# A hybrid encoder layer on one core: the first loads in wider pieces, four pool tiles accumulated together, stored tiles read back through POOL's queue

## The chip, the cores and the metric

The kernel runs on one core of one Trainium2 chip. The time is the device time of one execution in microseconds. A core has a matmul engine (TensorE, PE in the profile, with PEld for its weight loads), a vector engine (VectorE, DVE), a scalar engine (ScalarE, ACT), GpSimd (POOL) and SyncE (SP). In this kernel SP and POOL issue the transfers between DRAM and on-chip memory. Products accumulate in PSUM; a PSUM slot here holds 128 rows of 512 floats.

## The reference

One layer is computed for T = 384 tokens: 256 of one new stream and 8 x 16 of eight running streams. All data is float32.

```python
u = rmsnorm(x, g_mix_pre)
proj = u @ w_in                                  # pool | z | xBC | dt | gates
a_pool = pool_mixer(proj[pool])                  # windows 2, 4, 8, 16: mean minus self, then a map per group of 512
xbc = silu(causal_conv(proj[xBC]))
y, h = ssd_scan(xbc, softplus(proj[dt]))         # exact chunked scan
a_ssd = gated_rmsnorm(y + d_skip * x, z)
m = sigmoid(g_A) * (a_pool @ w_pool_proj) + sigmoid(g_B) * (a_ssd @ w_ssd_proj)
x = x + rmsnorm(m @ w_out, g_mix_post)
x = x + rmsnorm(relu(rmsnorm(x, g_mlp_pre) @ w_up)**2 @ w_down, g_mlp_post)
```

The model width is 2048 (KD = 16 tiles of 128), the SSD branch is 4096 wide in 8 groups, the MLP 8192. The new pool, convolution and SSM states are outputs as well.

## The kernel before

**Products in three parts.** A float32 product is made of three products in a rounded format: each operand is split into a rounded high part `h` (ScalarE, an activation with Copy) and the rest `l` (VectorE, a subtraction), and `mm3` (L75) adds h·h, h·l and l·h. So each weight piece passes one transfer on SP, one split on ScalarE, one on VectorE, and then TensorE.

**Weight units.** `wfetch` (L59) brings one unit, 128 rows of 1024 floats (512 KB), `wsplit` (L64) splits it. The pool `wpool` has three buffers each for the raw unit, its high and its low part. `proj` (L104) makes one tile of 128 output columns x 384 tokens from two units, in the two `mmtile` slots of PSUM; `moving` (L110) makes three token blocks x 512 output columns in three of the six `sstile` slots, from units of 18 products of 512 columns each. `take` (L95) hands out a split unit: as long as the list `queue` isn't empty, it keeps three split units in `ready`, so that a split is ordered two units ahead of its use; with an empty list it orders load and split where they are used.

**What sets the order.** The framework orders the instructions of each engine when the program is built, by the order of the code as priority and by when its model says that an instruction can run. On the chip each engine then takes its own list strictly in that order, and waits on semaphores. `behind` pins single instructions behind others. Tiles of one name share a fixed number of slots; a new tile waits until the old one has been read for the last time.

**The opening (L196 to L312).** Eight products on zeros (`NWARM`, L200) run while the first loads are on their way. x is loaded transposed, one tile of 128 x 384 for each k (`xload`, L213), the weights of the first three pool tiles as `w_e`, 384 columns for each k (`eload`, L208): k=0 and k=1 alone, then pairs, through the weight buffers of `wpool`. `xsplit` (L239) splits x times the norm's gain, `esplit` (L252) the weights, and `eprod` (L263) adds the products of k into three PSUM slots. The fourth pool tile, `ps3`, is then made from two ordinary units (`f0`, `f1`). x is loaded a second time by tokens (`tload`) for the row norms: three squares on ScalarE, three Newton steps on VectorE, and two products (`bc_x`, L309) that spread the norms over the partitions; ScalarE copies them to `rstd` (L311). Until then no pool tile can leave PSUM.

**The pooling stage (L329 to L496).** `pool_tile` reads a tile from PSUM, scales it by `rstd`, forms the window sums on VectorE, and splits the result. `pool_map` multiplies four of these tiles by the group's weights. Between them stand the first gates (`gate_a`): the first is made after the pool tile (1, 0). Here is the order:

```python
for gi in range(4):
    for k4 in range(4):
        pool_tile(gi, k4)
        if gi and k4 == 0:
            if gi == 1:
                sg = gate_a(0)
            pool_map(gi - 1, last[0])
```

The gated results `ma_scr` and the second gates `gb_scr` go to DRAM through POOL's queue, as do the 32 tiles of the SSD branch, `a_scr` (L783).

**The SSD groups (L792 to L881)** take their units, and those of the second gates (`w_gb`), from `queue`, which L796 and L797 fill.

**The branch projection, the merge and the output (L883 to L1091).** While the last two gates (`gate_b(2)` and `gate_b(3)`, L917) run, `aload` (L907) is called after each unit: it brings two tiles of `a_scr` back through SP's queue into three buffers named `ar`, and splits them on ScalarE (L913) and VectorE (L914). Then, for each of four blocks of 512 columns, `ma_scr` and `gb_scr` are read back through SP's queue (L925, L926), the branch is projected with 16 units of `w_ssd`, and the three are merged. `w_out` follows with 8 units for each block; in its last block five units have buffers of their own.

**The MLP (L1094 to L1251)** ends with `w_down`. `moving`'s arguments `tail` and `own` there: in the very last block all four units are used block by block (`tail` = 4), and one of them is split into buffers of its own rather than into those of `wpool` (`own` = 1). The last block of tokens is then normed, added to x and stored (L1223 to L1241).

Of the kernel before, what the change touches and what calls it, by code (L numbers as in the profile page):

```python
# [6 lines left out]
F32 = mybir.dt.float32  # L7
F32R = mybir.dt.float32r
# [6 lines left out]
P = 128  # L15
# [10 lines left out]
MAGIC = 1597463007.0  # L26
NWARM = 8

# [5 lines left out]
def build(ctx, tc, io):  # L34
# [148 lines left out]
    def in_units(i):  # L183
        return [win[i - 4, 0], win[i - 4, 1]]

# [10 lines left out]
    warm = pa.tile([P, 512], mybir.dt.bfloat16, name="warm", bufs=1)  # L196
    gp.memset(warm, 0.0)
    gp.memset(onesr.bitcast(F32), 1.0)
# [3 lines left out]

    x0 = pa.tile([P, KD + T], F32, name="x0g", bufs=1)
    sy.dma_start(x0, io["x0g"])
# [12 lines left out]

# [14 lines left out]
    f0 = wfetch(in_units(4)[0], "p3_0")  # L232
    sy.dma_start(ident, io["cst"][:, C_IDENT : C_IDENT + P])
    tload(2)
    f1 = wfetch(in_units(4)[1], "p3_1")
    sy.dma_start(cst[:, P:], io["cst"][:, P:])
    sy.dma_start(vec, io["vec"])

    def xsplit(k):  # L239
        x = xr[k]  # L240
        h = xgp.tile([P, T], F32R, name=f"xgh{k}")
        l = xgp.tile([P, T], F32R, name=f"xgl{k}")
        g1 = x0[:, k : k + 1]
        s.activation(h, x, AF.Copy, scale=g1)
        v.scalar_tensor_tensor(out=l, in0=x, scalar=g1, in1=h.bitcast(F32), op0=ALU.mult, op1=ALU.subtract)
        xg.append((h, l))

    early = [sstile(f"pj_p{n}")[:, :T] for n in range(3)]

    turn = [None]  # L250

    def esplit(k):  # L252
        w, n = eu[k]
        h = wpool.tile([P, 1024], F32R, tag="wh", name=f"wh_e{k}")[:, : n * T]
        l = wpool.tile([P, 1024], F32R, tag="wl", name=f"wl_e{k}")[:, : n * T]
        if k == 0:
            v.tensor_copy(h, w)
        else:
            turn[0] = s.activation(h, w, AF.Copy)
        v.tensor_tensor(l, w, h.bitcast(F32), ALU.subtract)  # L260
        return h, l

    def eprod(k, j, hl):  # L263
        h, l = hl
        col = lambda n: slice(j * T + n * P, j * T + n * P + P)
        xh, xl = xg[k]
        if k == 0:
            for a, b in ((h, xh), (h, xl), (l, xh)):
                for n in range(3):
                    te.matmul(early[n], a[:, col(n)], b, start=a is h and b is xh, stop=False)  # L270
            return
        for n in range(3):
            last[0] = mm3(early[n], h[:, col(n)], l[:, col(n)], xh, xl, False, k == KD - 1)
# [6 lines left out]

    for k in (0, 1):
        hl = esplit(k) if k == 0 else None
        xsplit(k)
        eprod(k, 0, hl or esplit(k))
    for k in range(2, KD, 2):
        xsplit(k)
        xsplit(k + 1)
        hl = esplit(k)
        eprod(k, 0, hl)
        eprod(k + 1, 1, hl)  # L290
        if k in (10, 14):
            square((k - 10) // 4, turn[0])
    ps3 = sstile("pj_p3")[:, :T]
    early.append(ps3)
    half(ps3, 0, wsplit(f0), xg)
    square(2, None)
    half(ps3, 1, wsplit(f1), xg)
    dgh = pa.tile([P, 3, P], F32R, name="dgh", bufs=1)
# [17 lines left out]
    with tc.tile_pool(name="phc", bufs=1, reuse_waits="tile") as pc, tc.tile_pool(name="phc2", bufs=2, reuse_waits="tile") as pc2:  # L316
# [192 lines left out]
    with tc.tile_pool(name="phd", bufs=2, reuse_waits="tile") as pd, tc.tile_pool(  # L509
# [391 lines left out]
    with ExitStack() as phe:  # L901
        pe1 = phe.enter_context(tc.tile_pool(name="phe", bufs=1, reuse_waits="tile"))
        pe2 = phe.enter_context(tc.tile_pool(name="phe2", bufs=3, reuse_waits="tile"))
        pe4 = phe.enter_context(tc.tile_pool(name="phe4", bufs=1, reuse_waits="tile"))
        ab = []

        def aload():  # L907
            for i in (len(ab), len(ab) + 1):
                a = pe2.tile([P, T], F32, tag="ar", name=f"ar{i}")
                sy.dma_start(a, a_scr[i])  # L910
                h = pe1.tile([P, T], F32R, name=f"abh{i}")
                l = pe1.tile([P, T], F32R, name=f"abl{i}")
                s.activation(h, a, AF.Copy)  # L913
# [278 lines left out]
    with tc.tile_pool(name="phg", bufs=1, reuse_waits="tile") as pg, tc.tile_pool(  # L1192
# [9 lines left out]
        for c8 in range(NC):  # L1202
# [12 lines left out]
            for nb in range(4):  # L1215
                o = [sstile(f"wd{c8}_{nb}_{b}") for b in range(3)]

                def done(b):
# [154 lines left out]
```

## Time and profile before

| | |
|---|---|
| three runs, median (lowest to highest) | 2807.32 us (2806.77 to 2808.29) |
| the profiled execution | 2807.07 us |
| its span in the profile | 2804.9 us |
| mean granted clock of TensorE | 0.999 |
| read from DRAM, written | 407.11 MB, 41.72 MB |

The profile shows one execution. Times are microseconds from the span's start unless marked ns. A row of the timeline gives start, duration, engine, line of the kernel, operation, output and inputs, shapes, how many were merged into the row, and in brackets how long the engine was idle ahead of it and what ended that. Rows of waits give the waiting engine and line, whom it waited for, the total in us, how often and the longest. A row of groups gives the count, the busy time, the mean in ns of one, and the idle time ahead. A row of transfers gives the issuing queue, the count, the size of one and the median time from issue to landing. A row of stretches gives start and end, length, then for each engine the busy time and the instructions, then granted clock, busy share of the transfer engines and GB/s. Ends of products are modelled, so rows of PE overlap; the distance of two starts is what a product costs.

### The profile page before, as it was taken

How to read it: one execution, taken by the hardware profiler on the slowest of the kernel's cores; microseconds unless marked ns; L12 is line 12 of the kernel's file. 1: busy time of each engine (PE TensorE's matmuls, PEld its weight loads, DVE VectorE, ACT ScalarE, POOL GpSimd, SP SyncE). 2: the span in 40 equal slices, each digit the busy share in tenths (PEclk: the TensorE clock that was granted, in tenths of full speed). 3: DMA queues.
4: the chain of work that ended last, by engine and by line, in shares of the span. 5: the costliest groups of instructions: out<-in, count | busy, mean ns of one | idle time of the engine just before them, and what ended most of it. 6: DMA issues, size and time to landing. Idle time of an engine off the chain costs nothing.

```text
span 2804.9 us, 38300 instructions
## 1 busy us (share of the span) xinstructions
PE 2792.9 (100%) x15271; PEld 2542.6 (91%) x15271; DVE 1501.4 (54%) x1979; ACT 1173.4 (42%) x1822; POOL 105.8 (4%) x143
## 2 busy tenths in 40 slices
PE   9999999999999999999999999999999999999998
PEld 8998889999999999988888888989899898989897
DVE  6575335677787778756333336434444444444446
ACT  5443225556565656544322235433233332323233
POOL 0000000001010101010000000000000000000000
PEclk9999999999999999999999999999999999999999
DMA  7444445556665566657544544443444443444443
GB/s 272 131 124 150 139 139 199 186 182 207 197 228 192 201 198 223 197 186 233 175 146 161 176 144 131 130 131 125 131 126 129 127 130 126 129 128 128 130 127 124
DMA packets 148355, 451.35 MB, mean 161 GB/s; under 512 B 18064, under 2 KB 49104, under 8 KB 143184
## 3 DMA queue, kind: packets, MB, share of 16 engines
q1 hardware_dynamic: 140048, 412.97, 45.9%
q0 software_dynamic: 8128, 35.93, 3.3%
q8 instruction: 120, 1.97, 0.3%
q14 instruction: 59, 0.48, 0.1%
HBM read 407.11 MB, written 41.72 MB: 160 GB/s over the span
## 4 chain that ended last, share of the span: by engine, by line
PE 98%; ACT 1%; DMA 0%; DVE 0%; issue 0%; SPq 0%; DVEq 0%; ACTq 0%
PE pj_up L77 6%; PE pj_up L78 6%; PE pj_up L76 6%; PE wd L120 6%; PE wd L118 6%; PE wd L119 6%; PE pj_x L76 5%; PE pj_x L78 4%; PE pj_x L77 4%; PE pj_z L76 3%; PE pj_z L77 3%; PE pj_z L78 3%; PE pj_sp L119 3%; PE pj_sp L120 3%; PE pj_sp L118 3%; PE pj_gb L118 2%
## 5 line engine op out<-in xcount | busy, mean ns | idle before, releaser
L77 PE MATMUL pj_up<-x1l,wh_up 128*128 128x384 f32 (+1 forms) x1032 | 343.9, 333 | 0.6 <-DVE x1l L1041 0.6
L76 PE MATMUL pj_up<-x1h,wh_up 128*128 128x384 f32 (+1 forms) x1032 | 344.0, 333 | 0.0
L78 PE MATMUL pj_up<-x1h,wl_up 128*128 128x384 f32 (+1 forms) x1032 | 343.9, 333 | 0.0
L120 PE MATMUL wd<-wh_wd,hl 128*128 128x512 f32 x762 | 296.6, 389 | 0.0
L119 PE MATMUL wd<-wl_wd,hh 128*128 128x512 f32 x762 | 296.6, 389 | 0.0
L118 PE MATMUL wd<-wh_wd,hh 128*128 128x512 f32 x762 | 296.3, 389 | 0.0
L69 DVE TENSOR_TENSOR wl_wd<-w_wd,wh_wd 128x1024 fp32r<-128x1024 f32 x127 | 155.7, 1226 | 261.9 <-ACT wh_wd L68 261.9
L68 ACT ACTIVATE wh_wd<-w_wd 128x1024 fp32r<-128x1024 f32 x127 | 134.8, 1061 | 350.8 <-PE wd L120 284.2
L68 ACT ACTIVATE wh_up<-w_up 128x1024 fp32r<-128x1024 f32 x126 | 133.7, 1061 | 322.1 <-PE pj_up L77 258.0
L69 DVE TENSOR_TENSOR wl_up<-w_up,wh_up 128x1024 fp32r<-128x1024 f32 x126 | 154.4, 1226 | 198.1 <-ACT wh_up L68 198.0
L76 PE MATMUL pj_x<-xgh,wh_x 128*128 128x384 f32 x768 | 258.2, 336 | 0.0
L77 PE MATMUL pj_x<-xgl,wh_x 128*128 128x384 f32 x768 | 256.6, 334 | 0.0
L78 PE MATMUL pj_x<-xgh,wl_x 128*128 128x384 f32 x768 | 256.6, 334 | 0.0
L77 PEld LDWEIGHTS pj_up<-x1l,wh_up 128*128 128x128 f32 x1032 | 193.8, 188 | 1.0 <-DVE x1l L1041 0.7
L76 PEld LDWEIGHTS pj_up<-x1h,wh_up 128*128 128x128 f32 x1032 | 193.7, 188 | 0.3
L78 PEld LDWEIGHTS pj_up<-x1h,wl_up 128*128 128x128 f32 x1032 | 193.8, 188 | 0.0
L78 PE MATMUL pj_z<-xgh,wl_z 128*128 128x384 f32 x512 | 171.0, 334 | 0.0
L76 PE MATMUL pj_z<-xgh,wh_z 128*128 128x384 f32 x512 | 171.0, 334 | 0.0
L77 PE MATMUL pj_z<-xgl,wh_z 128*128 128x384 f32 x512 | 171.0, 334 | 0.0
L120 PEld LDWEIGHTS wd<-wh_wd,hl 128*128 128x128 f32 x762 | 143.0, 188 | 29.8
L119 PEld LDWEIGHTS wd<-wl_wd,hh 128*128 128x128 f32 x762 | 143.0, 188 | 29.7
L118 PEld LDWEIGHTS wd<-wh_wd,hh 128*128 128x128 f32 x762 | 143.0, 188 | 29.4
(319 smaller groups left out, 5799.7 us busy)
## 6 DMA issues: line engine op xcount, KB each, us to landing
w_up<-w_up SPq DMA_DIRECT2D x128, 512.0 KB, 3.4
w_wd<-w_down SPq DMA_DIRECT2D x128, 512.0 KB, 3.4
w_x<-w_in SPq DMA_DIRECT2D x96, 512.0 KB, 3.8
w_z<-w_in SPq DMA_DIRECT2D x64, 512.0 KB, 3.9
w_sp<-w_ssd SPq DMA_DIRECT2D x64, 512.0 KB, 3.4
w_ga<-w_ga SPq DMA_DIRECT2D x32, 512.0 KB, 3.5
w_pp<-w_pp SPq DMA_DIRECT2D x32, 512.0 KB, 3.4
hs<-ssm SPq DMA_DIRECT2D x16, 1024.0 KB, 5.4
```

Of the source, the lines that this page charges most:

```text
L68: s.activation(h, w, AF.Copy)
L69: v.tensor_tensor(l, w, h.bitcast(F32), ALU.subtract)
L76: te.matmul(out, wh, xh, start=first, stop=False, **how)
L77: te.matmul(out, wh, xl, start=False, stop=False, **how)
L78: return te.matmul(out, wl, xh, start=False, stop=last, **how)
L118: te.matmul(o[b], mh, wh[:, c], start=k == 0, stop=False)
L119: te.matmul(o[b], mh, wl[:, c], start=False, stop=False)
L120: last[0] = te.matmul(o[b], ml, wh[:, c], start=False, stop=k == nk - 1)
```

## The change

It has five parts.

1. **Opening.** x and the first weights come in one array: for each k 384 columns of x and 512 weight columns, side by side in one row of 896 floats. k=0 is one array with the gains, brought by two transfers; k=1 to 3 have a transfer and a tile each; then two transfers fill one tile of two k. The tiles have places of their own and no longer use `wpool`. Seven products on zeros instead of eight; VectorE clears their operand instead of POOL. For k=0 VectorE makes the low part of x ahead of that of the weights.
2. **Pool tiles.** The opening adds into four PSUM slots instead of three; the tile that comes from two ordinary units is the fifth, `ps4`. The first gate and the first pool map move behind the pool tile (1, 1).
3. **Queue of the loads.** The `a_scr`, `ma_scr` and `gb_scr` tiles are read back through POOL's queue instead of SP's.
4. **Splits ahead.** The units of `w_ssd` and `w_out` (but for the last five) join `queue`.
5. **End.** Two units of the last `w_down` block have buffers of their own.

```diff
-NWARM = 8
+NWARM = 7
...
-        return [win[i - 4, 0], win[i - 4, 1]]
+        return [win[i - 5, 0], win[i - 5, 1]]
...
-    gp.memset(warm, 0.0)
+    XW = T + 512
+    x0 = pa.tile([P, 928], F32, name="x0g", bufs=1)[:, : KD + XW]
+    sy.dma_start(x0[:, : KD + T], io["xw0"][:, : KD + T])
+    sy.dma_start(x0[:, KD + T :], io["xw0"][:, KD + T :])
+    v.memset(warm, 0.0)
...
-    xr.append(x0[:, KD:])
-    eu, xs3 = {}, []
-
-    def eload(k, n):
-        w = wpool.tile([P, 1024], F32, tag="w", name=f"w_e{k}")[:, : n * T]
-        sy.dma_start(w.rearrange("p (k n) -> p k n", k=n), io["w_e"][k : k + n].rearrange("k p n -> p k n"))
-        eu[k] = w, n
-
-    def xload(k):
-        x = pa.tile([P, T], F32, name=f"x{k}", bufs=1)
-        sy.dma_start(x, io["xT"][k])
-        xr.append(x)
+    xr.append(x0[:, KD : KD + T])
+    eu, xs3 = {0: x0[:, KD + T :]}, []
+
+    def xload(k, n):
+        x = pa.tile([P, n, XW], F32, name=f"xw{k}", bufs=1)
+        for j in range(n):
+            sy.dma_start(x[:, j], io["xw"][k + j])
+            xr.append(x[:, j, :T])
+        eu[k] = x[:, 0, T:] if n == 1 else x[:, :, T:]
...
-    eload(0, 1)
-    xload(1)
-    eload(1, 1)
-    for k in range(2, KD, 2):
-        xload(k)
-        xload(k + 1)
-        eload(k, 2)
+    for k in (1, 2, 3):
+        xload(k, 1)
+    for k in range(4, KD, 2):
+        xload(k, 2)
         if k in (6, 10):
             tload(len(xs3))
...
-    early = [sstile(f"pj_p{n}")[:, :T] for n in range(3)]
+    early = [sstile(f"pj_p{n}")[:, :T] for n in range(4)]
...
+        xl = None
         if k == 0:
-            v.tensor_copy(h, w)
+            v.tensor_copy(hv, w)
+            xl = xsplit(0)
         else:
-            turn[0] = s.activation(h, w, AF.Copy)
-        v.tensor_tensor(l, w, h.bitcast(F32), ALU.subtract)
+            turn[0] = s.activation(hv, w, AF.Copy)
+        with behind(xl):
+            v.tensor_tensor(lv, w, hv.bitcast(F32), ALU.subtract)
...
-                for n in range(3):
+                for n in range(4):
                     te.matmul(early[n], a[:, col(n)], b, start=a is h and b is xh, stop=False)
...
-    for k in (0, 1):
-        hl = esplit(k) if k == 0 else None
-        xsplit(k)
-        eprod(k, 0, hl or esplit(k))
-    for k in range(2, KD, 2):
+    for k in range(4):
+        if k:
+            xsplit(k)
+        eprod(k, 0, esplit(k))
+    for k in range(4, KD, 2):
         xsplit(k)
         xsplit(k + 1)
...
-            ps = early[k] if k < 4 else proj(in_units(1 + k), xg, f"p{k}")
+            ps = early[k] if k < 5 else proj(in_units(1 + k), xg, f"p{k}")
...
-                if gi and k4 == 0:
+                if gi and k4 == (gi == 1):
...
+        queue.extend((io["w_ssd"][nb, kp], f"sp{nb}_{kp}") for nb in range(4) for kp in range(16))
+        queue.extend((io["w_out"][nb, kp], f"wo{nb}_{kp}") for nb in range(4) for kp in range(8 if nb < 3 else 3))
...
-                sy.dma_start(a, a_scr[i])
+                gp.dma_start(a, a_scr[i])
...
-            sy.dma_start(ma, ma_scr[nb])
-            sy.dma_start(gb, gb_scr[nb])
+            gp.dma_start(ma, ma_scr[nb])
+            gp.dma_start(gb, gb_scr[nb])
...
-                    1 if c8 == NC - 1 and nb == 3 else 0,
+                    2 if c8 == NC - 1 and nb == 3 else 0,
...
-    cols = [i * P for i in range(3, 16)]
+    cols = [i * P for i in range(4, 16)]
...
-        "x0g": np.concatenate([chan(a["g_mix_pre"][0]), xcat[:, :P].T], axis=1),
-        "w_e": np.ascontiguousarray(w_in[:, :T]).reshape(KD, P, T),
+        "xw0": np.concatenate([chan(a["g_mix_pre"][0]), xcat[:, :P].T, w_in[:P, :512]], axis=1),
+        "xw": np.concatenate([xcat.T.reshape(KD, P, T), w_in[:, :512].reshape(KD, P, 512)], axis=2),
```

More of the change, by code (lines that the diff above doesn't have):

```diff
@@ L201, in build @@
         te.matmul(wt, warm[:, :P], warm, start=True, stop=True)
-    x0 = pa.tile([P, KD + T], F32, name="x0g", bufs=1)
-    sy.dma_start(x0, io["x0g"])
-    xr.append(x0[:, KD:])
-    eu, xs3 = {}, []
-    def eload(k, n):
-        w = wpool.tile([P, 1024], F32, tag="w", name=f"w_e{k}")[:, : n * T]
-        sy.dma_start(w.rearrange("p (k n) -> p k n", k=n), io["w_e"][k : k + n].rearrange("k p n -> p k n"))
-        eu[k] = w, n
-    def xload(k):
-        x = pa.tile([P, T], F32, name=f"x{k}", bufs=1)
-        sy.dma_start(x, io["xT"][k])
-        xr.append(x)
+    xr.append(x0[:, KD : KD + T])
[6 more added lines that the diff above has]
+        eu[k] = x[:, 0, T:] if n == 1 else x[:, :, T:]
     def tload(b):
@@ L221, in tload @@
         xs3.append(x)
-    eload(0, 1)
-    xload(1)
-    eload(1, 1)
-    for k in range(2, KD, 2):
-        xload(k)
-        xload(k + 1)
-        eload(k, 2)
+    for k in (1, 2, 3):
+        xload(k, 1)
+    for k in range(4, KD, 2):
+        xload(k, 2)
         if k in (6, 10):
             tload(len(xs3))
-    f0 = wfetch(in_units(4)[0], "p3_0")
+    f0 = wfetch(in_units(5)[0], "p4_0")
     sy.dma_start(ident, io["cst"][:, C_IDENT : C_IDENT + P])
     tload(2)
-    f1 = wfetch(in_units(4)[1], "p3_1")
+    f1 = wfetch(in_units(5)[1], "p4_1")
     sy.dma_start(cst[:, P:], io["cst"][:, P:])
@@ L244, in xsplit @@
         s.activation(h, x, AF.Copy, scale=g1)
-        v.scalar_tensor_tensor(out=l, in0=x, scalar=g1, in1=h.bitcast(F32), op0=ALU.mult, op1=ALU.subtract)
         xg.append((h, l))
-    early = [sstile(f"pj_p{n}")[:, :T] for n in range(3)]
+        return v.scalar_tensor_tensor(
+            out=l, in0=x, scalar=g1, in1=h.bitcast(F32), op0=ALU.mult, op1=ALU.subtract
+        )
+    early = [sstile(f"pj_p{n}")[:, :T] for n in range(4)]
     turn = [None]
     def esplit(k):
-        w, n = eu[k]
-        h = wpool.tile([P, 1024], F32R, tag="wh", name=f"wh_e{k}")[:, : n * T]
-        l = wpool.tile([P, 1024], F32R, tag="wl", name=f"wl_e{k}")[:, : n * T]
+        w = eu[k]
+        n = 1 if k < 4 else 2
+        h = wpool.tile([P, 1024], F32R, tag="wh", name=f"wh_e{k}")[:, : n * 512]
+        l = wpool.tile([P, 1024], F32R, tag="wl", name=f"wl_e{k}")[:, : n * 512]
+        hv, lv = (h, l) if n == 1 else (a.rearrange("p (k n) -> p k n", k=2) for a in (h, l))
+        xl = None
         if k == 0:
-            v.tensor_copy(h, w)
-        else:
-            turn[0] = s.activation(h, w, AF.Copy)
-        v.tensor_tensor(l, w, h.bitcast(F32), ALU.subtract)
+            v.tensor_copy(hv, w)
+            xl = xsplit(0)
+        else:
+            turn[0] = s.activation(hv, w, AF.Copy)
+        with behind(xl):
+            v.tensor_tensor(lv, w, hv.bitcast(F32), ALU.subtract)
         return h, l
@@ L264, in eprod @@
         h, l = hl
-        col = lambda n: slice(j * T + n * P, j * T + n * P + P)
+        col = lambda n: slice(j * 512 + n * P, j * 512 + n * P + P)
         xh, xl = xg[k]
@@ L268, in eprod @@
             for a, b in ((h, xh), (h, xl), (l, xh)):
-                for n in range(3):
+                for n in range(4):
                     te.matmul(early[n], a[:, col(n)], b, start=a is h and b is xh, stop=False)
             return
-        for n in range(3):
+        for n in range(4):
             last[0] = mm3(early[n], h[:, col(n)], l[:, col(n)], xh, xl, False, k == KD - 1)
@@ L292, in build @@
             square((k - 10) // 4, turn[0])
-    ps3 = sstile("pj_p3")[:, :T]
-    early.append(ps3)
-    half(ps3, 0, wsplit(f0), xg)
+    ps4 = sstile("pj_p4")[:, :T]
+    early.append(ps4)
+    half(ps4, 0, wsplit(f0), xg)
     square(2, None)
-    half(ps3, 1, wsplit(f1), xg)
+    half(ps4, 1, wsplit(f1), xg)
     dgh = pa.tile([P, 3, P], F32R, name="dgh", bufs=1)
```

1 line of the change is left out of this document (removed).

## The prediction

> **What bounds the kernel now.** I read the page first, then the waits of TensorE, then busy time by stage.
>
> ```profile
> span 2804.9 us, 38300 instructions
> ...
> PE 2792.9 (100%) x15271; PEld 2542.6 (91%) x15271; DVE 1501.4 (54%) x1979; ACT 1173.4 (42%) x1822; POOL 105.8 (4%) x143
> ...
> PE 98%; ACT 1%; DMA 0%; DVE 0%; issue 0%; SPq 0%; DVEq 0%; ACTq 0%
> ```
>
> TensorE (PE) carries 98% of the chain that ended last. A busy PE could still be a slow one, so its waits come next, all of them longer than the profile's threshold:
>
> ```profile
> PE warm_o L201 <- POOL warm L197: 1.3, 1, 1.3
> PE pj_up L77 <- DVE x1l L1041: 0.6, 1, 0.6
> PE trx L587 <- ACT xs L544: 0.5, 1, 0.5
> PE pj_p L76 <- ACT wh_e L259: 0.5, 1, 0.5
> ```
>
> That is 2.9 us in all. Only the first and the last lie in code that the change touches. By stage (start:end, length, then busy us of PE, PEld, DVE, ACT, POOL):
>
> ```profile
> 4.30:48.70 44.40, 43.85 (x244) 42.65 (x243) 29.61 (x57) 28.38 (x44) 1.93 (x5) 1.00 0.93 346
> ...
> 41.00:250.00 209.00, 209.00 (x1116) 196.25 (x1115) 140.47 (x250) 84.72 (x144) 10.24 (x19) 1.00 0.46 140
> ...
> 1270.00:1336.00 66.00, 66.00 (x292) 54.48 (x291) 43.30 (x63) 34.46 (x54) 5.01 (x10) 1.00 0.75 239
> 1336.00:1620.00 284.00, 284.00 (x1278) 235.73 (x1277) 106.02 (x107) 80.87 (x88) 1.62 (x3) 1.00 0.50 167
> ```
>
> In the pooling stage (41 to 250), in the last gates (1270 to 1336) and in the branch projections (1336 to 1620) PE has no hole at all. Edits there can only lose time. What can be won is in the first 48.7 us, and, behind PE's last product, in the tail.
>
> The change neither adds nor removes a product of the computation: 192 + 48 products of 384 columns make the first five pool tiles in both kernels, only grouped differently. One warm-up product goes.
>
> **The opening, the only term that should count.** PE pays 0.173 us per product at full pace (47.68 to 47.85 in the timeline), and the first product of the gate, which closes the stage, starts at 48.72:
>
> ```profile
> 0.74 0.52 POOL L197 MEMSET warm<- 128x512 bf16 x1 [0.29 <-POOLq L1351]
> 1.32 3.60 PE L201 MATMUL warm_o<-warm 128*128 128x512 bf16 x8 [1.32 <-POOL warm L197]
> 3.71 0.36 DVE L257 CAST wh_e<-w_e 128x384 fp32r<-128x384 f32 x1 [3.71 <-DMA w_e<-w_e]
> 4.36 1.50 PE L270 MATMUL pj_p<-xgh,wh_e 128*128 128x384 f32 x3
> 5.68 0.72 PE L270 MATMUL pj_p<-xgl,wh_e 128*128 128x384 f32 x3
> 5.88 0.62 ACT L244 ACTIVATE xgh<-x,x0g 128x384 fp32r<-128x384 f32 x1 [1.98 <-DMA x<-xT]
> 6.40 0.52 ACT L259 ACTIVATE wh_e<-w_e 128x384 fp32r<-128x384 f32 x1
> 7.67 0.44 PE L78 MATMUL pj_p<-xgh,wl_e 128*128 128x384 f32 x1
> 9.64 0.44 PE L76 MATMUL pj_p<-xgh,wh_e 128*128 128x384 f32 x1 [0.48 <-ACT wh_e L259]
> 47.68 0.33 PE L76 MATMUL pj_p<-xgh,wh_p 128*128 128x384 f32 x1
> 47.85 0.33 PE L77 MATMUL pj_p<-xgl,wh_p 128*128 128x384 f32 x1
> 48.72 0.39 PE L118 MATMUL pj_ga<-wh_ga,xgh 128*128 128x512 f32 x1
> ```
>
> From the first real product (4.36) to the gate (48.72) stand 240 products and two for the row norms, 242 x 0.173 = 41.9 us, in 44.4 us. So 2.5 us are lost now: three slow first products (4.36 to 5.68, 0.44 each, 0.8 too much), and 1.7 of waits for the splits of k=1 and k=2 (around 7.67 and 9.64), whose operands arrive in transfers of 192 and 384 KB.
>
> First product. It needs the first weights landed and rounded (3.71 + 0.36 = 4.07), and the warm-ups done. The weight transfer grows from 384 to 512 columns (192 to 256 KB), the cast in proportion to 0.48: some 0.3 us later, 4.4. The warm-ups become seven (3.60 x 7/8 = 3.15 us) and their memset goes from POOL to VectorE, for which no row exists; between nothing and POOL's 0.52 us they end at 3.9 to 4.5. Start unchanged at about 4.4; bounds 0.3 earlier, 0.3 later.
>
> Slow products: four are now in the first group, 4 x (0.44 - 0.17) = 1.1 us lost.
>
> k=0 to k=1. Twelve products instead of nine run on k=0, so PE is done with it at 4.4 + 4 x 0.44 + 8 x 0.173 = 7.5. For k=1 one transfer of 448 KB must land, then ScalarE rounds x (0.62) and 512 weight columns (0.52 x 4/3, less its fixed part: 0.63), 1.3 us with the semaphores. Before, x of k=1 was there at 5.88, with 584 KB asked for up to it (rows of 400, 384 and 384 floats); now 904 KB are (400, 512 and 896). The rate of this stretch, 346 GB/s in its row, puts the extra 320 KB at 0.9 us: landed at 6.8, ready at 8.1, a hole of 0.6 us. The bound on the good side: what had been asked for behind x was on its way at 5.88 too, so the larger transfer may be no later, and the hole is 0. On the bad side all 1.7 us of waits come back. I take 0.4, nearer to what the rate gives. The third product of each column group also waits for the low part of the weights, as at 7.67: 0.3 us once.
>
> After that a k step costs PE 12 x 0.173 = 2.1 us and the wire 448 KB / 346 = 1.3 us, ScalarE 0.62 + 0.63, VectorE about the same: PE is never caught again, so the 9.64 hole is gone. Loss 1.1 + 0.4 + 0.3 = 1.8 against 2.5: **a gain of 0.7 us**, from a gain of 1.4 (hole 0, start 0.3 early) to a loss of 0.6 (1.1 + 1.7 lost, start 0.3 late). The tiles no longer go through the shared weight buffers, which also frees the transfer queue of their waits; that is off PE's path.
>
> [...]
>
> **Four tiles in flight, gate moved one tile later.** p0 to p4 now hold five of the six PSUM slots until the row norms exist, some 8 us later than now; the gate needs three. In both kernels one projection (48 x 0.173 = 8.3 us) runs between norms and gate, and VectorE reads two tiles in the first 1.2 us of it (41.10 to 42.25 here), so with the norms' own slot three are free in time: cost 0. But VectorE has tile chains and the gate's weight splits to do in turn:
>
> ```profile
> 41.10 0.43 DVE L336 TENSOR_TENSOR pbuf<-pj_p,rstd 128x256 f32<-128x256 f32 x1 [0.70 <-ACT rstd L311]
> ...
> 41.97 0.28 DVE L337 TENSOR_TENSOR pbuf<-pj_p,rstd 128x128 f32<-128x128 f32 x1
> ...
> 56.27 1.22 DVE L69 TENSOR_TENSOR wl_ga<-w_ga,wh_ga 128x1024 fp32r<-128x1024 f32 x1
> 58.48 1.22 DVE L69 TENSOR_TENSOR wl_ga<-w_ga,wh_ga 128x1024 fp32r<-128x1024 f32 x1
> ...
> L352 DVE TENSOR_TENSOR win<-pbuf 128x518 f32<-128x518 f32 x5 | 3.4, 693 | 0.0
> L372 DVE TENSOR_TENSOR dl<-d,dh 128x384 fp32r<-128x384 f32 x4 | 2.1, 550 | 0.0
> L355 DVE SCALAR_TENSOR_TENSOR d<-win,pbuf 128x256 f32<-128x256 f32 x5 | 2.1, 421 | 0.0
> L336 DVE TENSOR_TENSOR pbuf<-pj_p,rstd 128x256 f32<-128x256 f32 x5 | 2.1, 418 | 0.7 <-ACT rstd L311 0.7
> ```
>
> A gate unit is 18 products; by the row of the branch projections one lasts 284 / (1278 / 18) = 4.0 us. The fourth and fifth units start at 48.7 + 3 x 4.0 = 60.7 and 64.7; their splits end at 57.5 and 59.7, 3.2 and 5.0 us early. The sixth tile's chain now stands ahead of them: 0.42 + 2 x 0.69 + 0.42 + 0.55, and the small pieces (some 0.9), 3.7 us. Its last step must wait for the pool map anyway, which leaves 3.1. Just covered by the lead of 3.2: 0; with that last step ahead too, 0.5 us lost. Below nothing it can't go, since 41 to 250 has no hole.
>
> **Stored tiles through POOL's queue.** 32 activation loads (192 KB) and eight of the merge move from SP's to POOL's queue:
>
> ```profile
> L910 SPq DMA_DIRECT2D ar<-a_scr x32: 319/320/933, 1232.3 to 1329.3; - x32
> L913 ACT ACTIVATE abh<-ar x32: 503/525/527, 1283.5 to 1332.9; 128x384 fp32r<-128x384 f32 x32
> ...
> DMA to landing us min/median/max: 2.9/3.6/5.0
> ```
>
> ```profile
> 1336.19 1.70 POOL L505 DMA_DIRECT2D gb_scr<-gbt  x3 [29.33 <-ACT gbt L504]
> ...
> a_scr<-zs POOLq DMA_DIRECT2D x32, 192.0 KB, 2.5
> ...
> gb_scr<-gbt POOLq DMA_DIRECT2D x12, 256.0 KB, 4.7
> ```
>
> SP issues one in 0.32 us, POOL in 1.70 / 3 = 0.57. SP loses 32 x 0.32 = 10 us of issuing and its waits on their buffers; what stood behind, the weight transfers, starts earlier, but PE had no hole there: gain 0. On POOL the loads queue behind the gate's stores, which wait up to 29 us for a sigmoid, and behind them only the last gate's stores and the merge's loads. Who waits is ScalarE: it takes the loads in its fixed order between the weight splits, and PE waits for these. Now 32 loads pass in 1332.9 - 1283.5 + 0.5 = 49.9 us, 4.7 for each round of the three buffers. POOL adds 0.25 to a round, and the landing, for which the trace has no load of this size from POOL, lies between 2.5 and 4.7 (POOL's stores) against 3.6: a round of 3.85 to 6.05. I take 4.95, with the landing of the same loads on SP. Of 66 / 4.0 = 16 gate units, some 12 run beside the loads, 2.7 loads each: a unit then needs 2.7 / 3 x 4.95 = 4.45 us of rounds against PE's 4.0, 0.45 x 12 = 5.4 us behind at the end. Splits run up to two units ahead, 8 us less the split itself (1.2 on VectorE, taken as 1.1 on ScalarE): 5.7 us of cover. So 0; the far end is rival 1. The merge's eight loads stand behind them with a block of 16 units, 64 us, to spare.
>
> **Weights split two units ahead.** It moves the orders of 64 + 27 transfers and splits forward by two units; their three buffers stay, so a split still can't run before PE leaves the unit three back. In 1336 to 1620 PE waits for none: 0. Its one use is at the seam, 1336, where the first branch split now stands before the last loads; a lag of the loads at the seam then holds up nothing, since a branch unit uses only two of the 32.
>
> **Two own buffers in the last block.** The split of its third unit no longer waits for a shared buffer:
>
> ```profile
> 2781.19 1.22 DVE L69 TENSOR_TENSOR wl_wd<-w_wd,wh_wd 128x1024 fp32r<-128x1024 f32 x1
> ...
> 2795.97 0.69 DVE L1223 TENSOR_TENSOR hacc<-wd,hacc 128x512 f32<-128x512 f32 x1 [0.18 <-PE wd L120]
> ```
>
> PE waited for nothing here (its four waits are above), and the chain from 2795.97 to the span's end, 8.9 us, is untouched. Gain 0; bounds 0.2 either way, a sixth of a split.
>
> **Sum.** The profiled execution took 2807.07 us (span 2804.9 and 2.2 around it), 0.25 under the median of the three runs, 2807.32. Minus 0.7 gives 2806.4 and 2806.6: **2806.5 us**. The opening's own bounds make that 2805.8 to 2807.8.
>
> **Rivals.**
> 1. *The loads on POOL starve the weight splits; slower.* Place: 1283 to 1336. For it: ScalarE already waited 20.9 us for these loads, and it decides from 4.0 + 5.7 / 12 = 4.48 us per unit, a round of 4.97, right beside the one I take. Against it: this counts the order of before, and now two branch splits are ordered ahead of the last loads. With a landing of 4.15, halfway to the stores' 4.7, the round is 5.5, a unit 4.95, and 0.95 x 12 - 5.7 = 5.7 us are lost: **2812.2**; with 4.7 it is 6.05, 5.45, and 11.7 us, 2818. Chance 0.12.
>
> ```profile
> ACT abh L913 <- DMA ar<-a_scr: 20.9, 17, 2.5
> ```
>
> [...]
> 2. *The opening gives it back.* The single 448 KB transfer lands late and the hole of k=1 is as large as both were: 0.6 us lost at worst, none at best, **2807.5**. For it: x at 5.88 was the latest operand of all. Against: two holes become one. Chance 0.17.
> 3. [...] Chance 0.06.
> 4. *More gain:* hole 0, start 0.3 earlier, seam and the pooling stage cleaner: **2805.0**. Chance 0.06. Nothing brings 5.6 us: the opening loses 2.5, and the 8.9 us behind PE stay.
>
> **How the numbers follow.** Forecast 0.59, rivals 0.12, 0.17, 0.06, 0.06. The likeliest case has 2805.8 to 2807.8. No change is within 0.2%, 5.6 us (what a measurement of this kernel can tell): 2801.7 to 2812.9. Half of rival 1 and 0.01 for what I didn't see lie above: slower 0.07. Faster 0.02, for what I didn't see. Same 0.91. The range goes to rival 4 and to the lower half of rival 1: 2804.8 to 2810.5.
>
> **What would show it.** Opening right: the gate, now one projection later, starts at 48.72 + 8.3 - 0.7 = 56.3; one hole after k=0, none near 9.6. Rival 1: PE waits on `wh_gb` or `wl_gb` between 1283 and 1345, and loads landing later than 4 us. [...] Gate wrong: PE waiting on `wl_ga` between 60 and 75. The prediction is wrong if PE's waits outside the opening sum to over 1 us more than before.

## The result, and the profile after

The changed kernel takes 2811.55 us (median of 22 runs, 2809.98 to 2814.6), the kernel before 2807.69 (22 runs on the same chip, 2806.74 to 2808.84): 1.0014 times as long, 95% interval 1.0007 to 1.002. It is 3.9 us slower, where 2806.5 was forecast, and above the forecast range of 2804.8 to 2810.5. The page of the changed kernel, its span and its busy line:

```profile
span 2808.7 us, 38269 instructions
...
PE 2794.1 (99%) x15270; PEld 2542.1 (91%) x15270; DVE 1501.0 (53%) x1979; ACT 1176.0 (42%) x1821; POOL 126.7 (5%) x182
```

The span grew by 3.8 us and TensorE's (PE's) busy time by 1.2. A product behind a pause reads longer (0.44 us at 8.15, where one at full pace reads 0.33), so the busy sum does not say where the time went. The waits of PE between 1268 and 1345 do (us in total, times, longest), in a stage where the kernel before shows none:

```profile
PE pj_gb L119 <- DVE wl_gb L69: 1.3, 2, 0.8
PE pj_sp L119 <- DVE wl_sp L69: 0.8, 1, 0.8
PE pj_gb L118 <- ACT wh_gb L68: 0.3, 1, 0.3
```

The waits listed are only those above a threshold. The whole loss is read from two starts. From the third gate's first product to the first transposition of the merge PE took 1417.20 - 1270.12 = 147.08 us before and 1420.79 - 1269.48 = 151.31 after: **4.23 us lost in this stage**, which is more than the whole loss. Everywhere else the starts of PE's groups of products move by little: -0.2 us at the second pool map (123 us), -0.4 at the hole near 484, and nothing from 1421 to PE's last product; behind that the kernel takes 0.2 us longer. The same stage by windows, before (first row) and after (second row; busy PE, PEld, DVE, ACT, POOL):

```profile
1270.00:1336.00 66.00, 66.00 (x292) 54.48 (x291) 43.30 (x63) 34.46 (x54) 5.01 (x10) 1.00 0.75 239
```

```profile
1269.48:1335.48 66.00, 64.33 (x279) 51.67 (x279) 39.84 (x58) 30.78 (x48) 20.41 (x39) 1.00 0.72 231
```

In the same 66 us 13 products fewer are recorded; DVE and ACT did less too, so they were waiting, not overloaded. The activation loads, now on POOL:

```profile
L915 POOL DMA_DIRECT2D ar<-a_scr x32: 538/538/561, 1237.8 to 1332.7; - x32
L918 ACT ACTIVATE abh<-ar x32: 508/527/528, 1282.9 to 1336.5; 128x384 fp32r<-128x384 f32 x32
...
DMA to landing us min/median/max: 2.6/3.5/5.3
```

From issue to landing they are no slower than on SP (3.6). But all 32 pass ScalarE in 1336.5 - 1282.9 = 53.6 us instead of 1332.9 - 1283.5 = 49.4: 4.2 us more, just what PE lost. The timeline shows one place (start, duration, what ended the idle time):

```profile
1299.02 1.68 DVE L919 TENSOR_TENSOR abl<-ar,abh 128x384 fp32r<-128x384 f32 x3 [1.58 <-ACT abh L918]
1300.02 1.05 ACT L68 ACTIVATE wh_gb<-w_gb 128x1024 fp32r<-128x1024 f32 x1
1301.10 1.23 DVE L69 TENSOR_TENSOR wl_gb<-w_gb,wh_gb 128x1024 fp32r<-128x1024 f32 x1 [0.39 <-ACT wh_gb L68]
1302.46 1.60 POOL L915 DMA_DIRECT2D ar<-a_scr  x3 [5.77 <-DVE wl_gb L69]
1306.58 1.47 ACT L918 ACTIVATE abh<-ar 128x384 fp32r<-128x384 f32 x3 [5.51 <-DMA ar<-a_scr]
```

The first of the three `abl` ends at 1299.02 + 0.56 = 1299.58 and frees the buffer of the thirteenth load. That load is issued at 1302.46, 2.88 us later, where POOL otherwise takes 0.3 and SP took 0.03. ScalarE then waits 5.51 us for it, and the next weight split stands behind it. The row names `wl_gb` as the releaser, only because that ended last before the issue: the load's own wait is for `abl` and for the landing of the tenth load, which had the same buffer, at 1298.4.

### The profile page after: what moved, and what is told of

Its sections match the earlier page's. It is cut to its first block, busy times and chain, and to the rows that moved or that the text cites. A ratio compares the mean times of both kernels' runs of the same rounds, so it can differ in the third digit from the quotient of the medians.

```text
span 2808.7 us, 38269 instructions
## 1 busy us (share of the span) xinstructions
PE 2794.1 (99%) x15270; PEld 2542.1 (91%) x15270; DVE 1501.0 (53%) x1979; ACT 1176.0 (42%) x1821; POOL 126.7 (5%) x182
## 4 chain that ended last, share of the span: by engine, by line
PE 81%; issue 15%; DMA 2%; ACT 1%; POOL 1%; DVE 0%; POOLq 0%; SPq 0%; DVEq 0%; ACTq 0%
PE pj_up L78 6%; PE pj_up L77 6%; PE pj_up L76 6%; PE wd L120 6%; PE wd L119 6%; PE wd L118 6%; PE pj_x L76 4%; PE pj_x L77 4%; PE pj_x L78 4%; PE pj_z L77 3%; PE pj_z L78 3%; PE pj_z L76 3%; PE pj_sp L119 3%; PE pj_sp L120 3%; PE pj_sp L118 3%
```

## The experiments

Theory A: the loads' move to POOL is the loss. Rivals: the merge's loads or the weights ordered ahead (C), the order of the instructions around the late load (B). First the changed kernel once more, and three that undo or do one part. `a_ar_sp`, against the changed kernel:

```
-                gp.dma_start(a, a_scr[i])
+                sy.dma_start(a, a_scr[i])
```

> The changed kernel with only the 32 activation loads back on SP's queue; the merge's eight loads stay on POOL, and the two-units-ahead order stays. Theory A (the loads on POOL's queue are the loss): some 4.2 us come back, 2811.5 - 4.2 = 2807.3 us, and TensorE has no hole above 0.3 us between 1280 and 1345. Theory C (branch weights ordered ahead, or the merge's loads, bring it): the time stays at 2811 to 2812.

Measured: 2807.22 us against 2806.70 for the kernel before on the same chip (1.0, 0.9991 to 1.0009); the stage takes 146.91 us, nothing lost, and PE has no wait in it. `b_ar_pool`, the same line moved the other way in the kernel before:

```
-                sy.dma_start(a, a_scr[i])
+                gp.dma_start(a, a_scr[i])
```

> The kernel before with only the 32 activation loads moved to POOL's queue. Theory A: all of the loss comes with this one line, 2807.7 + 4.2 = 2811.9 us, with TensorE's holes between 1280 and 1345. Theory C: 2807.7, no hole. In between (2808.5 to 2810.5): the loads bring a part, and something else of the change adds to it.

Measured: 2810.13 us, 3.4 more than before (1.0014, 1.0005 to 1.0023); 149.55 us for the stage, 2.5 lost, with the waits on `wl_gb` and `wl_sp`. It is between the two expectations, 2808.5 to 2810.5, which was to mean that something else of the change adds to the loss; the loss that there is lies in the stage that A names. The profiled execution was the fastest of eleven, 2808.93 us, so its 2.5 us are rather too few. `a_noext`:

```
-        queue.extend((io["w_ssd"][nb, kp], f"sp{nb}_{kp}") for nb in range(4) for kp in range(16))
-        queue.extend((io["w_out"][nb, kp], f"wo{nb}_{kp}") for nb in range(4) for kp in range(8 if nb < 3 else 3))
+        pass
+        pass
```

> The changed kernel without the two lines that put the branch and output weights into the queue of weights taken two units ahead. Theory A: these lines give no cover at the seam, since ScalarE's order has the first branch split behind the last activation load with them and without them; the time is the changed kernel's, 2811.0 to 2812.0. Theory C (the lines bring the loss): 2807.3. Theory D (they did give cover): slower than the changed kernel by 1 us or more.

Measured: 2810.18 us (1.0013, 1.0004 to 1.0022), the stage 150.96 us, 3.9 lost. So C falls: the one line takes the whole loss back, and alone it makes most of it (3.4 us of 3.9 by the medians); the two-ahead order neither brings the loss nor covers it. The changed kernel again, `a_again`:

> The changed kernel once more, for a second profile. Theory A (the 32 activation loads on POOL's queue bring the loss, at one load that is issued 2.6 us late and at rounds that are some 0.4 us longer each): TensorE loses 3.5 to 5 us between 1280 and 1345 again, and since a late issue of a load is nothing that the program orders, the late load may be another one. Theory B (the order of the instructions is at fault, above all the three gate stores that stand between two loads): the same load is late by the same 2.6 us, and the holes of TensorE are the same to 0.1 us.

Measured: 2812.2 us, 5.2 lost in the stage. The holes differ from those of the first profile, against B, but the same load is late:

```profile
1298.55 0.56 DVE L919 TENSOR_TENSOR abl<-ar,abh 128x384 fp32r<-128x384 f32 x1 [0.90 <-ACT abh L918]
1299.98 1.04 DVE L919 TENSOR_TENSOR abl<-ar,abh 128x384 fp32r<-128x384 f32 x2 [0.87 <-ACT abh L918]
1301.41 1.23 DVE L69 TENSOR_TENSOR wl_gb<-w_gb,wh_gb 128x1024 fp32r<-128x1024 f32 x1 [0.39 <-ACT wh_gb L68]
1301.99 1.07 POOL L915 DMA_DIRECT2D ar<-a_scr  x2 [5.12 <-DVE abl L919]
```

1301.99 - 1299.11 = 2.88 us again, and here the issue falls in the middle of `wl_gb`, which so cannot be the releaser. In all four profiles with the loads on POOL it was the thirteenth, 2.88 us to 0.01. This is against A's guess that the late load may vary, and against B, since `b_ar_pool` has another order around it. Something counts. Two theories: POOL's instructions (F) or its transfers (G). Next come eight tiny instructions more (`a_pad_m8`), or four transfers more (`a_pad_d4`):

```
+    padm = consts.tile([P, 8], F32, name="padm")
...
+            [gp.memset(padm[:, i : i + 1], 0.0) for i in range(8 if g == 1 else 0)]
```

> The changed kernel with eight tiny memsets more on POOL at the start, nothing left out. In four profiles so far (the changed kernel twice, without the two-ahead lines, and the kernel before with the loads on POOL) the thirteenth activation load was issued 2.88 us after its buffer was free, to 0.01 us, where the others took 0.3. Theory F (POOL stalls at a place in its instruction stream, at so many instructions): eight instructions more, and a load is two, so the late load is now the ninth. Theory G (POOL stalls at so many transfers issued): no transfer is added, the thirteenth stays late by 2.88 us, and the time stays between 2810 and 2813.

```
+    pad_scr = [dram.tile([P, T], F32, name=f"pad_scr{i}") for i in range(4)]
...
                 gp.dma_start(a_scr[i], z)
+                1 <= D.g <= 1 and gp.dma_start(pad_scr[j], z)
```

> The changed kernel with four transfers more on POOL, near 700 us: the second group's four stored tiles are stored once more, to scratch. Theory G (a stall at so many transfers issued by POOL): the late load moves four places ahead, to the ninth, 2.88 us again, and the thirteenth takes 0.3. Theory F (so many instructions; these are four): the late load is the eleventh. Theory B (the order around the thirteenth): it stays the thirteenth.

Measured: with the memsets the thirteenth load stays late, by 2.87 us. The run took 2821.78 us, 10 us more than the changed kernel. In its trace the products of the first and second gates and of `w_out`, 1728 in all, start some 234 ns apart instead of 227 (between 1620 and 1730 us, mostly `w_out`, it has 480 products and the changed kernel 493), which makes about 11 us; why is not shown. So only the load's place is read from it. With four transfers more (2810.28 us) the ninth load is late: its `abl` was done at 1290.49 + 1.03 = 1291.52, its issue came at 1294.44, and the thirteenth took 0.3:

```profile
1290.49 1.03 DVE L919 TENSOR_TENSOR abl<-ar,abh 128x384 fp32r<-128x384 f32 x2 [0.27 <-ACT abh L918]
...
1294.44 0.55 POOL L915 DMA_DIRECT2D ar<-a_scr  x1 [2.56 <-DMA ar<-a_scr]
```

The landing that the row names as the releaser, the seventh load's, is not one that the ninth waits for: in the changed kernel's first profile the ninth was issued at 1291.4, before the seventh landed at 1293.5. F falls, G holds: it is the 114th transfer that POOL issues.

`a_ar_sp` shows the same far from these loads, which it has on SP. POOL issues 116 transfers there, and the 114th is the merge's last `gb_scr` load. Its buffer is free when `mar` ends, at 1536.86 + 0.69 = 1537.55, and it is issued 2.87 us later; in the changed kernel, where it is not the 114th, it takes 0.29. No engine waits for it:

```profile
1536.86 0.69 DVE L936 TENSOR_TENSOR mar<-mar,gbr 128x512 f32<-128x512 f32 x1
...
1540.42 0.54 POOL L931 DMA_DIRECT2D gbr<-gb_scr  x1 [54.65 <-DVE wl_sp L69]
```

`a_pad_r8` asks what is counted, with eight transfers of 16 rows each:

```
+                1 <= D.g <= 2 and gp.dma_start(pad_scr[j][:16], z[:16])
```

> The changed kernel with eight small transfers more on POOL: the first 16 of 128 rows of the stored tiles of groups 1 and 2 once more, eight times 24 KB, together the rows and bytes of one of the 192 KB stores. Theory G1 (the stall comes at a number of transfers, whatever their size): the late load is eight places ahead, the fifth. Theory G2 (it comes at a number of rows, bytes or descriptors): one place ahead, the twelfth.

```profile
1295.87 1.51 DVE L919 TENSOR_TENSOR abl<-ar,abh 128x384 fp32r<-128x384 f32 x3 [2.26 <-ACT abh L918]
...
1299.95 1.60 POOL L915 DMA_DIRECT2D ar<-a_scr  x3 [2.70 <-DVE wl_gb L69]
```

Measured: 2810.87 us, and the eleventh load is the late one: the second of the three `abl` ends at 1296.90, the issue comes 3.05 us later, 2.7 beyond the usual 0.3. That is two places ahead for eight small transfers. Neither theory had that number; it is near G2. Neither bytes nor packets set the place: ahead of the late transfer POOL's queue (`q0`; packets, MB, busy share) had moved this, in the changed kernel, `a_pad_r8` and `a_ar_sp`:

```profile
q0 software_dynamic: 8272, 35.67, 7.3%
```

```profile
q0 software_dynamic: 8400, 35.47, 7.3%
```

```profile
q0 software_dynamic: 8848, 39.60, 6.7%
```

What is counted, no run shows. As an estimate from these runs, a transfer of 16 rows counts for about a quarter of a full one (eight of them for two places), though it has an eighth of the rows and bytes.

Then the stall is pushed ahead of the loads by 24 full transfers (`a_pad_d24`):

```
+                1 <= D.g <= 6 and gp.dma_start(pad_scr[j], z)
```

> The changed kernel with 24 transfers more on POOL: the stored tiles of groups 1 to 6 are stored twice. Theory G: the stall falls before the first load of the rounds, where nothing waits for POOL; no load is more than 0.5 us late, TensorE loses some 2.5 us less between 1280 and 1345, and the time is 2807.5 to 2809 although POOL does more. Theory A as first put (each round is longer by POOL's later start and longer issue, and that is the loss): the time stays at 2810 to 2812.

```profile
1298.88 1.69 DVE L919 TENSOR_TENSOR abl<-ar,abh 128x384 fp32r<-128x384 f32 x3 [1.07 <-ACT abh L918]
1299.73 1.72 POOL L915 DMA_DIRECT2D ar<-a_scr  x3 [2.67 <-DVE abl L919]
```

Measured: the thirteenth load takes 0.3 us (1299.73 - 1299.44), and no load stalls; the eighteenth alone comes later, 2.0 us after its buffer is free, because it stands behind three gate stores. The stage takes 148.59 us, 1.5 lost instead of 4.2, and the kernel 2807.02 us against 2808.18 before (0.9998, 0.9989 to 1.0006). It stores 4.7 MB more than the changed kernel, and measures no slower than the kernel before. So the stall is worth some 2.7 us of the loss, by one profile each; the kernels with the stall lose from 2.5 to 5.2.

The stall is where theory G puts it, at POOL's 114th transfer. That is now a gate's first store: it comes 3.57 us after its sigmoid begins, where the same store in the changed kernel (second pair of rows) comes after 0.99, so it is 2.58 us late:

```profile
1231.73 2.05 ACT L507 ACTIVATE gbt<-pj_gb,yx 128x512 f32<-128x512 f32 x3 [0.36 <-PE pj_gb L120]
...
1235.30 1.63 POOL L508 DMA_DIRECT2D gb_scr<-gbt  x3 [24.68 <-ACT wh_gb L68]
```

```profile
1231.63 2.05 ACT L507 ACTIVATE gbt<-pj_gb,yx 128x512 f32<-128x512 f32 x3 [0.36 <-PE pj_gb L120]
...
1232.62 1.90 POOL L508 DMA_DIRECT2D gb_scr<-gbt  x3 [22.06 <-ACT gbt L507]
```

Two more kernels ask what else helps. First more buffers (`a_ar5`):

```
-        pe2 = phe.enter_context(tc.tile_pool(name="phe2", bufs=3, reuse_waits="tile"))
+        pe2 = phe.enter_context(tc.tile_pool(name="phe2", bufs=5, reuse_waits="tile"))
```

> The changed kernel with five buffers instead of three for the activation loads, which stay on POOL. If the loss is time that ScalarE waits for loads (by the stall or by the long rounds), five buffers cover 2.9 us: no hole of TensorE above 0.4 us between 1280 and 1345, and 2807 to 2808 us, as with the loads on SP. If the transfers themselves are slower on POOL's queue, or ScalarE's order is at fault, more buffers bring little: 2809.5 or more.

```profile
1293.56 1.05 ACT L68 ACTIVATE wh_gb<-w_gb 128x1024 fp32r<-128x1024 f32 x1
1295.77 1.05 ACT L918 ACTIVATE abh<-ar 128x384 fp32r<-128x384 f32 x2 [1.16 <-DMA ar<-a_scr]
1300.23 1.46 ACT L918 ACTIVATE abh<-ar 128x384 fp32r<-128x384 f32 x3 [3.41 <-DMA ar<-a_scr]
1301.60 1.04 ACT L68 ACTIVATE wh_gb<-w_gb 128x1024 fp32r<-128x1024 f32 x1
```

Measured: 2811.76 us (1.0013, 1.0004 to 1.0022), 4.4 lost. The loads were through by 1321.7 instead of 1336.5, but the order of ScalarE, which is made anew for each kernel, now puts five of them between two weight splits, and the splits are 8.0 us apart where PE needs one in 4.0. The thirteenth load is late here too, by 2.92 us. More buffers moved the waiting, they did not cover it. Next, the third gate's stores (`a_d24_st`, on top of the 24 stores):

```
-            gp.dma_start(gb_scr[nb][:, b], t[:, b])
+            (sy if nb == 2 else gp).dma_start(gb_scr[nb][:, b], t[:, b])
```

> The changed kernel with the 24 doubled stores (no stall among the loads) and with the third gate's three stores on SP's queue, so that on POOL no load stands behind a store. With the stall away, TensorE still lost 1.5 us between 1280 and 1345. Theory H (these 1.5 us come from the load that waits 1.7 us behind the three stores): at most 0.5 us is left, 2806 to 2807. Theory I (they come from POOL's later start and longer issue, 0.3 and 0.2 us for each wait, in every round): 1 to 1.5 us stay, and the time is that of the kernel with the 24 stores alone, to 0.5 us.

Measured: 148.65 us for the stage, 1.6 lost, as with the 24 stores alone: theory H falls. (The median is 2808.87 us or 1.0003, 0.9994 to 1.0012. The profiled execution, 2810.43, lost 1.8 us elsewhere: PE waits 2.3 us for ScalarE at 486 where it waited 0.5 before; that is not explained.)

```profile
486.47 0.55 PE L590 MATMUL trx<-cst,xs 128*128 128x128 f32 x3 [2.31 <-ACT xs L547]
```

At last the opening, alone in the kernel before (`b_open`, the changed kernel with all its other edits undone), and mended (`a_best`, the loads on SP as in `a_ar_sp`, and k=1 in two transfers):

> The kernel before with the new opening and the four pool tiles in flight alone; loads, merge, order of the branch weights and last block as before. My forecast for this part was a gain of 0.7 us. Theory K (one large transfer is late, as in the profiles of the changed kernel): the second pool map starts between 0.2 us earlier and 0.6 us later than before, and the time is the kernel before's to 0.6 us. Rival (the forecast was right, and another edit spoils the opening): 0.7 us earlier.

```
-            sy.dma_start(x[:, j], io["xw"][k + j])
+            for c in (slice(0, T), slice(T, XW)) if k == 1 else (slice(0, XW),):
+                sy.dma_start(x[:, j, c], io["xw"][k + j][:, c])
```

> The changed kernel with the activation loads back on SP, and with the second step's x and weights in two transfers (192 and 256 KB) instead of one of 448 KB. Over the profiles so far the new opening is worth from a gain of 0.2 to a loss of 0.6 us at the second pool map, not the gain of 0.7 forecast: ScalarE can begin to round x only when the whole 448 KB are there, at 7.0 to 7.7 us. Theory J (the one large transfer is what is late): x is there some 0.7 us earlier, only the weights' rounding (0.6 us) is left after the second transfer, TensorE's hole behind the first step shrinks by 0.5 us, and the second pool map starts 0.2 to 0.8 us earlier than in the kernel before. Rival (the wire is the limit, and the hole stays): no earlier than 0.1 us, and 2807.2 as with the loads on SP alone.

Measured: `b_open` starts the second pool map 0.35 us earlier than before and takes 2806.62 against 2807.35 us (0.9997, 0.9988 to 1.0006); `a_best` starts it 0.49 us earlier, and takes 2806.37 against 2808.27 (0.9995, 0.9986 to 1.0004). Neither is told apart from the kernel before; `a_best` beats the changed kernel. k=1 in the changed kernel's second profile, then in `a_best`:

```profile
7.71 0.61 ACT L240 ACTIVATE xgh<-xw,x0g 128x384 fp32r<-128x384 f32 x1 [3.85 <-DMA xw<-xw]
8.23 0.61 ACT L261 ACTIVATE wh_e<-xw 128x512 fp32r<-128x512 f32 x1
...
8.90 0.44 PE L76 MATMUL pj_p<-xgh,wh_e 128*128 128x384 f32 x1 [1.77 <-ACT wh_e L261]
```

```profile
5.53 0.62 ACT L241 ACTIVATE xgh<-xw,x0g 128x384 fp32r<-128x384 f32 x1 [1.64 <-DMA xw<-xw]
...
7.18 0.63 ACT L262 ACTIVATE wh_e<-xw 128x512 fp32r<-128x512 f32 x1 [1.04 <-DMA xw<-xw]
...
7.86 0.45 PE L76 MATMUL pj_p<-xgh,wh_e 128*128 128x384 f32 x1 [1.04 <-ACT wh_e L262]
```

In two transfers x is there at 5.53 instead of 6.8 to 7.7, its rounding is over when the weights land at 7.18, and the first product of k=1 starts at 7.86 instead of 7.98 to 8.92. That is theory J for the landing and for the second pool map; PE's hole behind k=0, 1.04 us, is no shorter than the others' mean, so the gain of half a microsecond rests on one profile.

One table answers to all of it: how long the loads pass ScalarE (last `abh` start less the first), and how long the stage lasts, both over the kernel before (49.4 and 147.08 us).

| kernel | loads on | loads pass, us | over before | stage over before |
|---|---|---|---|---|
| a_ar_sp | SP | 48.9 | -0.5 | -0.2 |
| a_best | SP | 48.9 | -0.5 | -0.2 |
| b_open | SP | 50.6 | 1.2 | 1.3 |
| a_pad_d24 | POOL, stall earlier | 50.9 | 1.5 | 1.5 |
| a_d24_st | POOL, stall earlier | 50.9 | 1.5 | 1.6 |
| b_ar_pool | POOL | 51.8 | 2.4 | 2.5 |
| a_pad_d4 | POOL | 52.6 | 3.2 | 3.3 |
| a_noext | POOL | 53.2 | 3.8 | 3.9 |
| changed | POOL | 53.6 | 4.2 | 4.2 |
| a_pad_r8 | POOL | 53.7 | 4.3 | 4.3 |
| a_again | POOL | 54.6 | 5.2 | 5.2 |

The rows behind two of them, `a_ar_sp` and `a_pad_d24`:

```profile
L918 ACT ACTIVATE abh<-ar x32: 505/525/527, 1283.3 to 1332.2; 128x384 fp32r<-128x384 f32 x32
```

```profile
L918 ACT ACTIVATE abh<-ar x32: 506/525/527, 1283.0 to 1333.9; 128x384 fp32r<-128x384 f32 x32
```

Every microsecond that the loads take beyond the 49.4 of before is a microsecond of PE's: the stage had no cover left. (Not in the table are `a_ar5`, whose order is another, and `a_pad_m8`, whose slower products lengthen the stage: 54.0, 4.6 and 5.0.) What POOL's later and longer issue costs without the stall cannot be told to better than 0.3 to 2 us: the loads on SP themselves passed in 48.9 to 50.6. The slowest of these, `b_open`, lost 1.3 us with a median landing of 3.8 us instead of 3.6, nearly as much as the 1.5 on POOL without the stall. ScalarE's order around the third gate's sigmoids also differs between the kernels with the loads on SP and on POOL; no run separates that.

## Why the prediction was wrong

**Stored tiles through POOL's queue: the step that failed, twice.** The first failure is "5.7 us of cover" against 5.4 us behind. By the same sum the kernel before, with 49.4 / (31 / 3) = 4.78 a round, 4.30 a unit, was already 12 x 0.30 = 3.6 us behind, and any more was lost: the real cover is what before used, some 3.7 us (5.2 - 1.5 with the 24 stores, 8.0 - 4.2 in the changed kernel, whose round is 5.19). I took splits two units ahead from the program and subtracted their durations; the check was at hand, since the sum could be put to the kernel before and asked what it leaves. The longer rounds cost 1.5 us in the two kernels without the stall among the loads; how much of that is POOL's, and how much the spread that `b_open` shows on SP, is open.

The second failure is a term that the sum does not have: the stall at POOL's 114th transfer, the other 2.7 us. Nothing in the trace of before showed it, since POOL issues only 108 transfers there.

The landing came as taken, that of SP (median 3.5 against 3.6). The round of 4.95 us came out too, 50.9 / (31 / 3) = 4.93 without the stall, but by luck: I read 4.7 for the kernel before, where it is 4.78, and added 0.25, where 0.15 was measured. The sign named for a wrong prediction came: PE's waits outside the opening grew by over 1 us, with 2.4 in this stage.

**Weights split two units ahead.** The forecast of 0 stands (`a_noext`: no gain, no loss), but its use at the seam was argued wrongly: I read from the program that the first branch split would stand ahead of the last loads. ScalarE's order, made anew, has it behind them, with the lines and without:

```profile
1336.50 0.53 ACT L918 ACTIVATE abh<-ar 128x384 fp32r<-128x384 f32 x1 [0.37 <-DMA ar<-a_scr]
1336.93 1.99 ACT L68 ACTIVATE wh_sp<-w_sp 128x1024 fp32r<-128x1024 f32 x2
```

So it could not help against rival 1, of which it was the chief argument.

**Opening: right in kind, mis-sized.** The changed kernel's first profile:

```profile
4.21 0.43 DVE L258 CAST wh_e<-x0g 128x512 fp32r<-128x512 f32 x1 [3.07 <-DMA x0g<-xw]
4.78 1.43 PE L273 MATMUL pj_p<-xgh,wh_e 128*128 128x384 f32 x4 [0.41 <-DVE wh_e L258]
...
6.96 0.62 ACT L240 ACTIVATE xgh<-xw,x0g 128x384 fp32r<-128x384 f32 x1 [3.10 <-DMA xw<-xw]
...
8.15 0.44 PE L76 MATMUL pj_p<-xgh,wh_e 128*128 128x384 f32 x1 [0.52 <-ACT wh_e L261]
...
8.89 0.44 PE L78 MATMUL pj_p<-xgh,wl_e 128*128 128x384 f32 x1
```

One hole behind k=0, the wait for the low part (8.89) and no hole at 9.6 came as forecast, and a few slow first products, though from one to seven of them where four were taken, at 0.24 to 0.46 us instead of 0.17. What sets their number, no run shows, so nothing measured is behind the third rival's 0.06. But the first product started at 4.78 instead of 4.4, and over the ten profiles with this opening (all but `a_pad_m8`) at 4.43 to 4.79, 4.57 on average; PE waited 0.3 to 2.1 us behind k=0, 1.0 on average, instead of 0.4. The gate started at 56.84 instead of 56.3: a gain of 0.2, and over the ten profiles a mean loss of 0.15 at the second pool map (0.35 gained to 0.6 lost). That is rival 2, as far as it goes. The terms that were too small are the start and the landing of the one 448 KB transfer: ScalarE could begin on it at 7.3 us on average, where 6.8 was taken.

**Right:** four tiles in flight and the later gate cost 0 (PE's shift is the same from the gate to the second pool map, and no wait on `wl_ga`); two own buffers, 0 (the shift is 3.59 us at the merge's first transposition and at PE's last product); the chain behind PE's last product takes 9.5 us, before 9.4.

**Rival 1** had the place, the kind of wait and nearly the time (2812.2 against 2811.55), with a chance of 0.12. Its sign, loads landing later than 4 us, did not come: the time is lost ahead of the issue, where I had looked for nothing. So the number is luck: 2812.2 was worked out from a slower landing that no run shows. The landing after the issue is no longer (median 3.5 us against 3.6), and what is longer is the step from a free buffer to the issue, 0.3 us against 0.03, and the issue, 0.54 against 0.32.

## What to carry to other kernels

When a stage shows no wait, work out how far its slowest feeder is from causing one, and put the sum first to the kernel as it is: a cover that it already uses is not there for the change. Loads on which an in-order engine waits, as ScalarE here did for 5.51 us with a weight split behind, belong on a queue that answers at once; here POOL's queue added a later answer to every round (0.3 us against SP's 0.03), and a rare stall of its own (2.6 us, once). Deeper buffers or an order written further ahead help only where the order that each engine really gets shows it.

## What the hardware showed that I had not expected

POOL's queue stops once, for 2.6 us beyond its usual 0.3, at the 114th transfer of these kernels. That is the thirteenth load in every kernel with the same transfers ahead of it, the ninth with four more, a gate's store with 24 more, and the merge's last load, 240 us later, when the activation loads are on SP. With eight transfers of 16 rows ahead of it, it is the 120th. In the kernel before POOL issues 108 and does not get that far. POOL answered a freed buffer in 0.29 to 0.30 us, SP in 0.03. And the same opening, ten times, began its second pool map between 122.68 and 123.61 us: the transfers of the first 8 us land up to 0.9 us apart from one kernel to the next (k=1 at 6.8 to 7.7), and after the same seven warm-ups one to seven products run below full pace (0.24 to 0.46 us instead of 0.17). Each is more than the opening was worth.
